# Feed-forward taps that read PSUM, and 33 up-projection blocks multiplied unsplit in fp32 in the first pass

## The chip, the core and the metric

The kernel runs on one core of a Trainium2 chip. The metric is the device time of one execution, in microseconds. A core has five engines with instruction streams of their own: TensorE (PE: matmuls, and PEld: the loads of their stationary operand), VectorE (DVE), ScalarE (ACT), GpSimd (POOL) and SyncE (SP), which here issues all DMAs. TensorE writes its sums to PSUM, in banks of 512 fp32 columns; the other operands stand in SBUF.

## What is computed

One layer of a hybrid decoder for a prompt of 2048 tokens and 8 sample sequences of 8 tokens, all in fp32, with width 1024. A mixing part (convolutions and a gated delta rule) is followed by the feed-forward part that the change is about:

```
up, ffn_buf_new = _causal_dwconv(_rmsnorm(x, norm_ffn_g) @ w_up, ffn_buf, ffn_conv_w, ffn_conv_b)
gate, val = jnp.split(up, 2, axis=-1)
x = x + (jax.nn.silu(gate) * val) @ w_down
```

`w_up` has 1024 x 5632 and `w_down` 2816 x 1024 elements. The causal convolution has 3 taps per channel: `y[t] = w2*u[t] + w1*u[t-1] + w0*u[t-2] + b`, where the two columns ahead of the first are a saved state (zero for the prompt's start).

## The kernel before

**Passes.** The prompt is cut into six passes of 256, 384, 384, 384, 384 and 256 tokens; the last one also carries the 64 sample tokens (320 columns). Activations lie transposed, channels on the 128 partitions and tokens in the columns. Each pass runs its input projection, mixing, `w_out`, norm, feed-forward part and per-layer gate; the mixing of the next pass (convolution steps `cacc`, the delta rule's chain) is merged into the feed-forward stretch of the one before. The position of a unit in that merged plan gives its priority; the final order on each engine and in SP's queue is drawn up when the kernel is built.

**Matmuls.** An fp32 product is made of three fp32r ones: weights and activations are split into a rounded half and the rest, and `gemm` multiplies high by high, high by low and low by high. A block of weights is 8 tiles of 128 x 128, so a `w_up` block takes 24 matmuls into one bank of the pool `g` (three banks), which `w_out`, `w_in`, `w_down` and the PLE gate use too.

**Weights.** `wblock` (L242) brings a block into one of three `w` tiles. The first time it loads it raw (0.5 MB) into a tile `raw`; `split` (L230) lets ScalarE copy the high half and GpSimd (for some `w_in` and `w_out` blocks VectorE) subtract it from the raw one; then the halves (1 MB) are stored to DRAM. Later passes load those halves. Half of the `w_up` and `w_down` blocks aren't stored at the first split but split again in the second pass and stored then (L250). `get` (L260) keeps three blocks ahead.

**Feed-forward.** `units_f` works on 44 blocks of `w_up` per pass, a gate and a value block in turn, and after each four of them on two blocks of `w_down` (four outputs of 128 channels each, 6 matmuls an output) of the group before. In `half` (L1211) GpSimd copies the two saved columns from `ffh` to the head of an SBUF tile `row`; the matmuls fill a bank; ScalarE copies the bank behind those two columns of `row`, and writes `y = w2*u + b` from the bank; GpSimd saves the last two columns of `row` to `ffh`; VectorE adds the two other taps to `y`, each a `scalar_tensor_tensor` of `row`, shifted by a column, with `y`. In the last pass the sample tokens go through a tile `srow` in the same way. `units_norm` (L1177) makes the normed activations: part by part VectorE writes `h`, and `split` turns it into the two halves of `hT2`.

**X.** The residual `X` has two buffers of a tag `X`, which the split input of the second pass also uses early on. Every pass loads its `X` from DRAM in `units_w` (L1161, the load in L1167).

Of the kernel before, what the change touches and what calls it, by code (L numbers as in the profile page):

```python
# [42 lines left out]
def step_kernel(  # L43
# [23 lines left out]
    def nm(s):  # L67
        uid[0] += 1
        return f"{s}_{uid[0]}"
# [10 lines left out]
    def gbank():  # L80
        return pg.tile([P, 512], F32, tag="g", name=nm("g"))
# [65 lines left out]
    def r_tile(tag, w=NMAX, dt=F32):  # L147
        return rp.tile([P, w], dt, tag=tag, name=nm(tag), bufs=3)

    def srow_tile():  # L150
        return rp.tile([P, NSQ, 38], F32, tag="srow", name=nm("srow"), bufs=2)

    def h_tile(name="h"):
        return rp.tile([P, 512], F32, tag="h", name=nm(name), bufs=2)
# [84 lines left out]
    def w_tile():  # L239
        return wp.tile([P, 2, KD, P], F32R, tag="w", name=nm("w"), bufs=3)  # L240

    def wblock(key, src, hi_e="a", lo_e="g", nk=KD):  # L242
        w = w_tile()
        if key in halves:
            SY.dma_start(w.bitcast(F32), halves[key])
        else:
            raw = raw_tile("raw")
            SY.dma_start(raw if nk == KD else raw.rearrange("p (k o) c -> p k (o c)", k=nk), src)
            split(raw, w[:, 0], w[:, 1], hi_e, lo_e)
            if key[0] in ("w_up", "down") and key not in seen and (key[1] // P + key[-1]) % 2:  # L250
                seen.add(key)
                return w[:, 0], w[:, 1]
            halves[key] = hw.tile([P, 2, KD, P], F32, tag=nm("halves"), name=nm("halves"))
            SY.dma_start(halves[key], w.bitcast(F32))
        return w[:, 0], w[:, 1]
# [32 lines left out]
    def halfs(a):  # L288
        return a[:, 0], a[:, 1]

    def gemm_w(ps, w, hT, c0, cw):
        gemm(ps, (lambda k: w[0][:, k, :], lambda k: w[1][:, k, :]),
             (lambda k: hT[0][:, k, c0:c0 + cw], lambda k: hT[1][:, k, c0:c0 + cw]), KD)
# [45 lines left out]
    def to_row(q, row, srow, r, ps, fn):  # L339
        for off, q0, ln in seg(q):  # L340
            if q0 is None:
                fn(srow[:, :, r:r + LSQ], sv(ps[:, off:off + ln]), off, ln)
            else:
                fn(row[:, r:r + ln], ps[:, off:off + ln], off, ln)
# [832 lines left out]
    def units_norm(q):  # L1177
        n = q.n

        def stats():  # L1180
            q.hT2 = big.tile([P, 2, KD, NMAX], F32R, tag="hT2", name=nm("hT2"))
            rs = token_rs(q.acc, q)
            q.dgs = []
            for t, c0, L in q.tiles:
                q.dgs.append(dp.tile([P, P], F32, tag="Zt", name=nm("dg"), bufs=ZB))
                ts(V, q.dgs[-1][:L, :L], ident[:L, :L], rs[:L, t:t + 1], MUL)

        def spread_rs():
            q.nps = ps = bank()
            for i, (t, c0, L) in enumerate(q.tiles):  # L1190
                mm(ps[:, c0:c0 + L], one1[:L, :], q.dgs[i][:L, :L], i == 0, i == len(q.tiles) - 1)

        def part(b):
            h = h_tile()
            stt(V, h[:, :n], q.X[:, b, 0:n], gains[:, b, 1:2], q.nps[:, :n], MUL, MUL)
            split(h[:, :n], q.hT2[:, 0, b, 0:n], q.hT2[:, 1, b, 0:n], "a", "v" if b % 2 else "g")
        return [((), stats), ((), spread_rs)] + [((), lambda b=b: part(b)) for b in range(KD)]


    def units_f(q):  # L1200
        n, np_, sam = q.n, q.np, q.sam
        out = []
        z = {}

        def begin():
            z["f"] = big.tile([P, 2 * FG * 2 * NMAX], F32R, tag="F", name=nm("fbuf"))
            if sam:
                z["st"] = big.tile([P, 2 * FT, 2 * NSQ], F32, tag="zs", name=nm("fst"))
                load_T("fst", [st_ffn[0].rearrange("s r c -> (s r) c")], 2 * DFF, z["st"])

        def half(col):  # L1211
            ffS = W["ff"]
            w = get()
            y = r_tile("y")
            row = r_tile("row", NMAX + 3)
            srow = srow_tile() if sam else None
            G.tensor_copy(row[:, 0:2], ffh[:, col, 0:2])  # L1217
            if sam:
                G.tensor_copy(srow[:, :, 0:2], z["st"][:, col, :].rearrange("p (s r) -> p s r", r=2))
            ps = gbank()  # L1220
            gemm_w(ps[:, :n], w, halfs(q.hT2), 0, n)
            to_row(q, row, srow, 2, ps, lambda o, i, *a: act(o, i))
            act(y[:, :n], ps[:, :n], AF.Identity, scale=ffS[:, col, 2:3], bias=ffS[:, col, 3:4])
            G.tensor_copy(ffh[:, col, 0:2], row[:, np_:np_ + 2])  # L1224
            if sam:
                G.tensor_copy(ffh[:, col, 2:18].rearrange("p (s r) -> p s r", r=2), srow[:, :, 8:10])
            for tap in (1, 0):
                for o, i in taps(q, y, row, srow, tap):
                    stt(V, o, i, ffS[:, col, tap:tap + 1], o, MUL, ADD)
            return y  # L1230

        def ff_ap(slot, hl, j, a, b):
            base = ((slot * FG + j) * 2 + hl) * NMAX
            return z["f"][:, base + a:base + b]

        def gate(f):
            z["g"] = y = half(f)
            act(y[:, :n], y[:, :n], AF.Silu)

        def val(f, slot, j):  # L1240
            y = half(FT + f)
            tt(V, y[:, :n], y[:, :n], z["g"][:, :n], MUL)
            split(y[:, :n], ff_ap(slot, 0, j, 0, n), ff_ap(slot, 1, j, 0, n))

        def down(nk, slot, i):
            w = get()
            m = KD // nk
            for o in range(m):
                ps = bank() if q.ip == 0 and o % 2 else gbank()
                gemm(ps[:, :n], (lambda k: w[0][:, k * m + o, :], lambda k: w[1][:, k * m + o, :]),  # L1250
                     (lambda k: ff_ap(slot, 0, k, 0, n), lambda k: ff_ap(slot, 1, k, 0, n)), nk)
                xs = q.X[:, i * m + o, 0:n]
                tt(V, xs, xs, ps[:, :n], ADD)

        out.append(((), begin))
        pend = []
        for g0 in range(0, FT, FG):
            slot = (g0 // FG) % 2
            nk = min(FG, FT - g0)
            for j in range(nk):  # L1260
                f = g0 + j
                out.append(((("w_up", f * P),), lambda f=f: gate(f)))
                out.append(((("w_up", (FT + f) * P),), lambda f=f, slot=slot, j=j: val(f, slot, j)))
            out += pend
            pend = [((("down", g0, i),), lambda nk=nk, slot=slot, i=i: down(nk, slot, i)) for i in range(nk)]
        return out + pend
# [191 lines left out]
```

## Time and profile before

| | us |
|---|---|
| median of 3 runs | 3202.05 |
| lowest, highest | 3193.27, 3202.27 |
| the profiled execution | 3196.92 |
| its span, first to last instruction | 3195.2 |

The profile is of one execution. The page gives busy time by engine; the trace behind it can be asked for stretches of the span, for groups of instructions by line, shape and operation, for waits and for the order of time. A group's line reads: line of the code, engine, operation, tile written <- tiles read, partitions x columns written <- read, count | busy us, mean ns of one | idle us of the engine before them, and what ended it. L96, L105 and L108 are helper lines (`stt`, `tt`, `act`), so the tiles' names tell instructions apart. The feed-forward stretches of the six passes begin at about 345, 785, 1335, 1852, 2368 and 2884 us. TensorE's granted clock is given as a share of 2.4 GHz, as a mean over its two levels, 1.2 and 2.4 GHz.

### The profile page before, as it was taken

What the parts mean: (1) busy time and instruction counts of PE and PEld (TensorE: products, weight loads), DVE (VectorE), ACT (ScalarE), POOL (GpSimd) and SP (SyncE); (2) the same over time, 40 slices, a digit from 0 to 9 for tenths busy, and PEclk for the clock granted to TensorE, in tenths of its full rate; (3) what the DMA queues carried; (4) which work ended last, traced back from release to release, by engine and by line L of the source; (5) the groups of instructions that cost most, each with busy time, mean ns of one, the idle gap of its engine ahead of it and who ended that gap; (6) DMA issues with size and microseconds to landing.
All of it is one profiled execution on the core that took longest, in us unless ns stands there. A gap on an engine that the chain in (4) does not pass through costs nothing.

```text
span 3195.2 us, 51070 instructions
## 1 busy us (share of the span) xinstructions
PE 2973.2 (93%) x18682; PEld 2900.9 (91%) x18682; DVE 2213.8 (69%) x5378; ACT 1122.4 (35%) x2473; POOL 894.5 (28%) x1518
## 2 busy tenths in 40 slices
PE   5979688777999999999999999999999999998998
PEld 5979678677999998999999999999999999998998
DVE  6986889957669686756757666857577866743443
ACT  4333344334323334422234342223442232323223
POOL 3422576634333432211121121121131121111221
PEclk8989898888999999999999999999999999998999
DMA  7636766667777867667665677665767765666885
GB/s 231 203 118 225 239 194 214 185 214 250 297 251 248 271 231 259 237 240 249 228 220 214 237 253 245 228 239 198 249 242 255 261 241 198 219 222 226 301 293 207
DMA packets 291968, 745.28 MB, mean 233 GB/s; under 512 B 51241, under 2 KB 202282, under 8 KB 216575
## 3 DMA queue, kind: packets, MB, share of 16 engines
q1 hardware_dynamic: 291719, 742.03, 67.9%
q8 instruction: 148, 2.42, 0.3%
q14 instruction: 101, 0.83, 0.1%
HBM read 607.75 MB, written 134.57 MB: 232 GB/s over the span
## 4 chain that ended last, share of the span: by engine, by line
PE 64%; DVE 7%; DMA 3%; ACT 1%; issue 1%; SPq 0%; ACTq 0%; DVEq 0%
PE g L89 57%; PE d L89 3%; PE m L89 2%; DMA w<-halves 2%; DVE h L96 1%; PE d L93 1%; PE m L93 1%; DVE y L96 1%; DVE rt L105 1%; DVE hT L105 0%; DMA out_dram<-yt 0%; DVE cacc L96 0%; DVE sy L96 0%; DVE X L100 0%; DVE X L105 0%
## 5 line engine op out<-in xcount | busy, mean ns | idle before, releaser
L89 PE MATMUL g<-hT,w 128*128 128x384 f32 (+2 forms) x9840 | 1684.6, 329 | 38.7 <-ACT hT L108 9.3
L89 PEld LDWEIGHTS g<-hT,w 128*128 128x128 f32 x9840 | 1600.7, 192 | 49.9 <-ACT hT L108 11.0
L89 PE MATMUL g<-fbuf,w 128*128 128x384 f32 (+2 forms) x2904 | 549.4, 338 | 32.8 <-DVE X L105 15.2
L96 DVE SCALAR_TENSOR_TENSOR y<-row,ffS,y 128x384 f32<-128x384 f32 (+1 forms) x528 | 337.6, 639 | 301.8 <-ACT y L108 275.8
L89 PEld LDWEIGHTS g<-fbuf,w 128*128 128x128 f32 x2904 | 489.7, 194 | 43.3 <-DVE X L105 16.8
L96 DVE SCALAR_TENSOR_TENSOR cacc<-H,cfS,cacc 128x384 f32<-128x384 f32 (+1 forms) x696 | 487.4, 700 | 9.3 <-ACT cacc L108 3.0
L105 DVE TENSOR_TENSOR X<-X,g 128x384 f32<-128x384 f32 (+2 forms) x532 | 276.7, 524 | 228.1 <-PE g L89 225.9
L108 ACT ACTIVATE row<-g 128x384 f32<-128x384 f32 (+1 forms) x336 | 152.4, 454 | 598.5 <-PE g L89 594.2
L105 POOL TENSOR_TENSOR w<-raw,w 128x1024 fp32r<-128x1024 f32 x123 | 307.6, 2502 | 193.4 <-ACT w L108 169.9
L1224 POOL COPY ffh<-row 128x2 f32<-128x2 f32 x264 | 61.9, 235 | 594.4 <-ACT row L108 589.5
L89 PE MATMUL g<-x,w 128*128 128x384 f32 (+2 forms) x1152 | 204.1, 331 | 5.9 <-ACT w L108 4.6
L89 PE MATMUL g<-mx,w 128*128 128x384 f32 (+2 forms) x1152 | 193.9, 327 | 12.3 <-DMA w<-halves 9.5
L89 PEld LDWEIGHTS g<-mx,w 128*128 128x128 f32 x1152 | 186.7, 191 | 15.1 <-issue 4.7
L1217 POOL COPY row<-ffh 128x2 f32<-128x2 f32 x264 | 82.8, 314 | 418.2 <-DVE y L96 312.8
L89 PEld LDWEIGHTS g<-x,w 128*128 128x128 f32 x1152 | 192.1, 195 | 6.7 <-ACT w L108 5.0
L108 ACT ACTIVATE y<-g,ffS 128x384 f32<-128x384 f32 (+2 forms) x264 | 169.3, 641 | 0.1
L108 ACT ACTIVATE w<-raw 128x1024 fp32r<-128x1024 f32 x139 | 146.5, 1055 | 63.3 <-PE g L89 14.9
L105 POOL TENSOR_TENSOR fbuf<-y,fbuf 128x384 fp32r<-128x384 f32 (+2 forms) x132 | 136.4, 1034 | 115.0 <-ACT fbuf L108 111.5
L108 ACT ACTIVATE y<-y 128x384 f32<-128x384 f32 (+2 forms) x132 | 65.7, 498 | 217.7 <-DVE y L96 217.4
L108 ACT ACTIVATE fbuf<-y 128x384 fp32r<-128x384 f32 (+2 forms) x132 | 65.8, 498 | 213.5 <-DVE y L105 213.3
L96 DVE SCALAR_TENSOR_TENSOR H<-row,dnS,H 128x384 f32<-128x384 f32 (+1 forms) x144 | 92.8, 646 | 34.2 <-ACT H L108 33.2
L105 POOL TENSOR_TENSOR y<-row,y 128x256 fp32r<-128x256 f32 x48 | 36.2, 754 | 272.7 <-PE m L89 218.1
(338 smaller groups left out, 3291.1 us busy)
## 6 DMA issues: line engine op xcount, KB each, us to landing
w<-halves SPq DMA_DIRECT2D x477, 1024.0 KB
halves<-w SPq DMA_DIRECT2D x106, 1024.0 KB
raw<-in_w_up_dram SPq DMA_DIRECT2D x66, 512.0 KB
raw<-in_w_down_dram SPq DMA_DIRECT2D x33, 512.0 KB
raw<-in_w_in_dram SPq DMA_DIRECT2D x24, 512.0 KB
xt<-in_x_prompt_dram SPq DMA_DIRECT2D x16, 512.0 KB
xT<-xt SPq DMA_DIRECT2D x16, 512.0 KB
out_dram<-yt SPq DMA_DIRECT2D x16, 512.0 KB
```

The lines of the kernel that those rows point to most:

```text
L89: T.matmul(out, lhsT=lhsT, rhs=rhs, start=start, stop=stop, skip_group_check=skip)
L93: T.transpose(out, in_, ident[:k, :k])
L96: return e.scalar_tensor_tensor(out=out, in0=in0, scalar=scalar, in1=in1, op0=op0, op1=op1)
L105: e.tensor_tensor(out=out, in0=a, in1=b, op=op)
L108: A.activation(out, in_, f, **kw)
L1217: G.tensor_copy(row[:, 0:2], ffh[:, col, 0:2])
L1224: G.tensor_copy(ffh[:, col, 0:2], row[:, np_:np_ + 2])
```

## The change

Three things change together.

- `wblock`: in the first pass the `w_up` blocks whose number isn't a multiple of 4 (33 of 44) are loaded raw into a `w` tile and handed on as they are. The other 11, and all `w_down` blocks, are split and stored in the first pass; those 33 are split and stored in the second. No block is split twice any more.
- `units_norm` and `up_gemm`: in the first pass the normed activations are also kept whole, in a tile `hf` of the tag `X`, and an unsplit block is multiplied with them by 8 fp32 matmuls.
- `half`: the bank holds two more columns ahead of the result, which ScalarE fills from `ffh`. VectorE's taps of the prompt columns read the bank, shifted by a column, and `row` is gone. ScalarE saves the last two columns to `ffh` after the taps. Sample columns still go through `srow`.

```diff
     def wblock(key, src, hi_e="a", lo_e="g", nk=KD):
+        if key[0] == "w_up" and key[1] // P % 4 and key not in seen:
+            seen.add(key)
+            w = wp.tile([P, KD, P], F32, tag="w", name=nm("w"), bufs=3)
+            SY.dma_start(w, src)
+            return w
         w = w_tile()
...
             split(raw, w[:, 0], w[:, 1], hi_e, lo_e)
-            if key[0] in ("w_up", "down") and key not in seen and (key[1] // P + key[-1]) % 2:
-                seen.add(key)
-                return w[:, 0], w[:, 1]
             halves[key] = hw.tile([P, 2, KD, P], F32, tag=nm("halves"), name=nm("halves"))
...
         def part(b):
-            h = h_tile()
+            if q.ip == 0:
+                if b == 0:
+                    q.hf = big.tile([P, KD, n], F32, tag="X", name=nm("hf"), bufs=2)
+                h = q.hf[:, b]
+            else:
+                h = h_tile()
...
+        def up_gemm(ps, w):
+            if isinstance(w, tuple):
+                return gemm_w(ps, w, halfs(q.hT2), 0, n)
+            for k in range(KD):
+                mm(ps, w[:, k, :], q.hf[:, k, :], k == 0, k == KD - 1, skip=False)
+
         def half(col):
             ffS = W["ff"]
             w = get()
             y = r_tile("y")
-            row = r_tile("row", NMAX + 3)
-            srow = srow_tile() if sam else None
-            G.tensor_copy(row[:, 0:2], ffh[:, col, 0:2])
+            ps = gbank()
+            up_gemm(ps[:, 2:2 + n], w)
+            act(ps[:, 0:2], ffh[:, col, 0:2])
+            act(y[:, :n], ps[:, 2:2 + n], AF.Identity, scale=ffS[:, col, 2:3], bias=ffS[:, col, 3:4])
             if sam:
+                srow = srow_tile()
                 G.tensor_copy(srow[:, :, 0:2], z["st"][:, col, :].rearrange("p (s r) -> p s r", r=2))
-            ps = gbank()
-            gemm_w(ps[:, :n], w, halfs(q.hT2), 0, n)
-            to_row(q, row, srow, 2, ps, lambda o, i, *a: act(o, i))
-            act(y[:, :n], ps[:, :n], AF.Identity, scale=ffS[:, col, 2:3], bias=ffS[:, col, 3:4])
-            G.tensor_copy(ffh[:, col, 0:2], row[:, np_:np_ + 2])
-            if sam:
+                act(srow[:, :, 2:2 + LSQ], sv(ps[:, 2 + np_:2 + n]))
                 G.tensor_copy(ffh[:, col, 2:18].rearrange("p (s r) -> p s r", r=2), srow[:, :, 8:10])
             for tap in (1, 0):
-                for o, i in taps(q, y, row, srow, tap):
-                    stt(V, o, i, ffS[:, col, tap:tap + 1], o, MUL, ADD)
+                c = ffS[:, col, tap:tap + 1]
+                stt(V, y[:, 0:np_], ps[:, tap:tap + np_], c, y[:, 0:np_], MUL, ADD)
+                if sam:
+                    stt(V, sv(y[:, np_:n]), srow[:, :, tap:tap + LSQ], c, sv(y[:, np_:n]), MUL, ADD)
+            act(ffh[:, col, 0:2], ps[:, np_:np_ + 2])
             return y
```

## Rows read from the trace of the kernel before

**Rows 1.** The page, busy time by engine: us (share of the span) and instructions.

```profile
PE 2973.2 (93%) x18682; PEld 2900.9 (91%) x18682; DVE 2213.8 (69%) x5378; ACT 1122.4 (35%) x2473; POOL 894.5 (28%) x1518
```

**Rows 2.** Busy time by stretch: us, each engine (instructions), clock, DMA share, GB/s.

```profile
345.00:700.00 355.00, 273.13 (x1910) 259.24 (x1909) 320.23 (x547) 150.00 (x308) 222.98 (x215) 0.88 0.65 201
...
785.00:1224.00 439.00, 418.39 (x2489) 409.77 (x2487) 322.10 (x670) 159.57 (x317) 149.91 (x211) 0.98 0.74 256
...
1335.00:1743.00 408.00, 405.98 (x2465) 401.46 (x2464) 266.00 (x652) 128.86 (x282) 66.98 (x178) 1.00 0.67 233
```

**Rows 3.** Groups by shape in the stretch 345 to 700 us.

```profile
L105 POOL TENSOR_TENSOR w<-raw,w 128x1024 fp32r<-128x1024 f32 x63 | 158.4, 2518 | 38.2 <-ACT w L108 30.1 <-PE g L89 7.6
...
L96 DVE SCALAR_TENSOR_TENSOR cacc<-H,cfS,cacc 128x384 f32<-128x384 f32 x116 | 120.2, 1037 | 1.0
L96 DVE SCALAR_TENSOR_TENSOR y<-row,ffS,y 128x256 f32<-128x256 f32 x88 | 73.2, 831 | 9.0 <-ACT y L108 8.5
...
L105 DVE TENSOR_TENSOR X<-X,g 128x256 f32<-128x256 f32 x44 | 17.9, 410 | 4.8 <-PE g L89 4.8
...
L108 ACT ACTIVATE row<-g 128x256 f32<-128x256 f32 x44 | 16.5, 375 | 18.3 <-PE g L89 18.2
```

**Rows 4.** Groups by shape, VectorE, 1335 to 1743 us.

```profile
L96 DVE SCALAR_TENSOR_TENSOR cacc<-H,cfS,cacc 128x384 f32<-128x384 f32 x116 | 73.4, 632 | 2.0 <-ACT cacc L108 0.8
```

**Rows 5.** Groups by shape, VectorE, 2884 to 3125 us (the last pass).

```profile
L96 DVE SCALAR_TENSOR_TENSOR y<-row,ffS,y 128x256 f32<-128x256 f32 x86 | 42.0, 489 | 77.2 <-ACT y L108 61.1 <-POOL ffh L1226 16.1
```

**Rows 6.** Order of time: start us, us, engine, line, operation, tiles, count [idle before].

```profile
520.20 2.39 POOL L105 TENSOR_TENSOR w<-raw,w 128x1024 fp32r<-128x1024 f32 x1 [1.19 <-ACT w L108]
520.45 2.42 DVE L96 SCALAR_TENSOR_TENSOR y<-row,ffS,y 128x256 f32<-128x256 f32 x1
...
525.00 2.82 PE L89 MATMUL g<-hT,w 128*128 128x256 f32 x22
```

**Rows 7.** Groups by shape, the whole span: operations with a stream in PSUM.

```profile
L96 DVE SCALAR_TENSOR_TENSOR h<-X,gains,m 128x256 f32<-128x256 f32 x8 | 3.7, 478 | 2.0 <-PE m L89 1.1 <-POOL hT L105 0.7
...
L108 ACT ACTIVATE srow<-g 128x64 f32<-128x64 f32 x56 | 12.4, 221 | 0.2 <-DVE y L96 0.2
```

**Rows 8.** The tile kd: count, ns min/median/max, first and last start us, forms.

```profile
L89 PE MATMUL d<-kd,Lm x64: 377/379/767, 80.2 to 2391.1; 128*128 128x256 f32 x64
L105 DVE TENSOR_TENSOR kd<-Um,gg x32: 409/420/2461, 68.9 to 2388.6; 128x256 f32<-128x256 f32 x32
```

**Rows 9.** Order of time on TensorE, 294 to 298 us.

```profile
295.36 0.60 PE L89 MATMUL d<-kd,Lm 128*128 128x256 f32 x2
...
297.54 0.59 PE L89 MATMUL d<-kd,Lm 128*128 128x256 f32 x2
```

**Rows 10.** Waits, 345 to 700 us: engine and tile <- what it waited for: us, times, longest.

```profile
ACT y L108 <- DVE y L96: 60.2, 19, 6.1
...
PE g L89 <- POOL w L105: 11.1, 11, 2.9
```

**Rows 11.** Order of time in the last pass, where a w_down turn begins.

```profile
2974.49 1.92 PE L89 MATMUL g<-fbuf,w 128*128 128x320 f32 x12
...
2975.07 0.62 ACT L108 ACTIVATE y<-g,ffS 128x320 f32<-128x320 f32 x1
...
2975.57 0.49 DVE L105 TENSOR_TENSOR X<-X,g 128x320 f32<-128x320 f32 x1 [2.13 <-PE g L89]
...
2976.37 0.28 DVE L96 SCALAR_TENSOR_TENSOR y<-srow,ffS,y 128x64 f32<-128x64 f32 x1
...
2976.57 0.48 DVE L105 TENSOR_TENSOR X<-X,g 128x320 f32<-128x320 f32 x1
2976.97 0.48 DVE L96 SCALAR_TENSOR_TENSOR y<-row,ffS,y 128x256 f32<-128x256 f32 x1
```

**Rows 12.** Order of time in SP's queue, 293 to 297 us.

```profile
294.10 4.38 SPq L1167 DMA_DIRECT2D X<-xT  x2
```

**Rows 13.** The chain that ended last, in order of time, about 798 us.

```profile
797.97 4.28 DMA raw<-in_w_up_dram
```

## The prediction

> **What bounds the kernel now.** I read the page first: TensorE is busy in 93% of the span [rows 1]. That mean hides two kinds of stage, so I cut the span at the feed-forward stretches of the six passes. In the second and third of them (785 to 1224 us and 1335 to 1743 us) TensorE is busy for 418.4 of 439 us and for 406.0 of 408 us [rows 2]: those stretches last as long as their matmuls, and other engines' savings are worth nothing there unless TensorE waits for them. The first one, 345 to 700 us, is different: TensorE is busy for 273.1 of 355 us and VectorE for 320.2, at a granted clock of 0.88, that is, with part of the time at the lower of the two levels, 1.2 instead of 2.4 GHz [rows 2].
>
> Why is VectorE so busy there? In the groups of this stretch the convolution step of the next pass (cacc) has a mean of 1037 ns and the feed-forward tap (y<-row) one of 831 ns [rows 3]. The same shapes take 632 ns [rows 4] and 489 ns [rows 5] in later stretches, where GpSimd splits no weights. The timeline shows how: a tap that starts 0.25 us after GpSimd's subtraction of a weight split (2.39 us) lasts 2.42 us itself, until that subtraction is over [rows 6]. Not every operation suffers: the 44 additions X<-X,g, with one operand in PSUM, have a mean of 410 ns in the same stretch and none of that [rows 3]. So VectorE operations whose two streams both come from SBUF stand still while GpSimd subtracts, and those with one stream in PSUM don't. This first stretch is where the change acts.
>
> **The change part by part.** Per execution 99 blocks (66 of w_up, 33 of w_down) are loaded raw and 66 stored as halves, as before; the bytes don't change. What moves is who splits when. Before, the first pass splits 44+22 blocks and the second 22+11. After, the first splits 11+22 and the second 33+0. The second pass splits as many as before, and its DMAs are as many; the first pass has 33 splits fewer.
>
> *Stretched VectorE time in the first stretch.* Taps: 88 x (831-489) = 30.1 us. Convolution: 116 x (1037-632) = 47.0 us. Together 77.1 us by 66 splits, 1.17 us for each. With taps that read PSUM and half of the splits, 30.1 + 47.0/2 = 53.6 us go. But a split that now meets a tap may meet a convolution step after; if the 33 that remain stretch as much each, 33 x 1.17 = 38.6 us stay and 38.5 us go. I take the middle, 46 us, and keep both ends.
>
> *The tap itself.* No row shows this tap from PSUM. The nearest is h<-X,gains,m, the same operation with one stream in PSUM: 478 ns at 256 columns [rows 7], against 489 ns for the tap from SBUF [rows 5]. I count no difference. [...]
>
> *Matmuls.* 33 blocks of 24 matmuls become 8 unsplit fp32 products. Split ones: 22 matmuls at 256 columns take 2.82 us [rows 6]; an estimate of 0.28 us for the last one's own duration leaves 2.54/21 = 0.121 us from start to start, 2.9 us for a block. Unsplit fp32 products leave two records each: 32 tiles kd are written and 64 matmuls of 0.379 us read them [rows 8]. Two of these in a row take 0.60 or 0.59 us [rows 9], so 0.22 or 0.21 us from start to start. A block then takes 8 x 2 x 0.215 = 3.44 us: 0.54 us dearer, 33 x 0.54 = +18 us of TensorE. It lies beside VectorE's work: 273.1+18 = 291 us, and VectorE's side, below, still ends later. If that cover is gone, it costs 18 us.
>
> *GpSimd and ScalarE.* In the stretch 33 x 2.52 = 83 us of GpSimd go [rows 3], with ScalarE's copies ahead of them, and GpSimd's two small copies a block go in all passes. ScalarE loses the row copy (375 ns here [rows 3]) and gains two 2-column copies; the nearest row, a 64-column copy from PSUM, is 221 ns [rows 7], so 442 against 375: no difference that counts. TensorE waited for splits on GpSimd for 11.1 us in this stretch [rows 10]; I leave that in the range, since the matmuls that replace it are longer.
>
> *Waits that are added.* ScalarE copies the block's last two columns to ffh after VectorE's second tap, and the bank g is free only after that. Queued behind it on ScalarE are the next evacuations and SiLU; behind the bank is TensorE. In the last pass I follow it through: a w_down turn starts at 2974.49 and each of its outputs takes some 0.88 us, ScalarE's y ends at 2975.69, and the taps and two additions share VectorE [rows 11]. The bank would come free at about 2977.4, after VectorE's second tap of the prompt columns (2976.97 on) and one of the sample columns. The fifth output wants it at 2978.0; the third and fourth take the two other banks as their additions end, 2976.06 and 2977.05, against 2976.3 and 2977.15. It fits with about 0.1 to 0.2 us to spare. 11 such turns in 5 passes are 55; I count 4 us, and 0 to 15 us (0.28 us, one short tap in the way, for each) as the bounds.
>
> *The X buffer.* The unsplit h takes the buffer into which X of the second pass is loaded now at about 295 us, right behind that of the first [rows 12]. That load moves behind the last w_up block of the first pass, in SP's queue among the loads of the w_down and w_out blocks. One transfer of 0.5 MB took 4.28 us [rows 13], and this one is three times as large: some 7 to 13 us, with the last w_down blocks (8 outputs, 24 matmuls each) to hide it. I count nothing; uncovered, it is up to 7 us. Unsplit weights land straight in w: the same 4.28 us, against two blocks (5.8 us) of lead. Nothing, as long as that holds.
>
> **Sum.** The profiled execution took 3196.9 us (3195.2 of span and 1.7 around); the median is 3202.05, 0.16% above. First stretch: VectorE 320.2-46 = 274 us; with its 35 us of idle time kept, 309 instead of 355 us, against TensorE's 291. So -46. Second to sixth: +4. 3196.9-46+4 = **3155 us**.
>
> **The rivals.** *TensorE keeps its idle time.* In the first stretch it has 82 us of it, much behind the chain of the delta rule, which is latency and no load. If what VectorE saves only becomes idle time there, the fp32 matmuls add 18 us and the split waits give 11 us back: 3196.9+4+7 = 3208 at the very worst; halfway between that and the forecast, 3181. For it: TensorE's nominal work rises. Against it: VectorE's idle share is only a tenth.
>
> *Slower: banks wait for late taps.* In the first stretch VectorE lags: ScalarE's SiLU waited for taps 19 times, 60.2 us in all, 6.1 us at the longest [rows 10]. Today that lag doesn't reach TensorE, because a bank is free after ScalarE's two reads. After, the bank is held over the lag, and the copy of two columns waits in ScalarE's queue. It decides where the lag exceeds the two other banks' blocks, 5.8 us. If all of it turned into TensorE waits, +60: 3215. Against it: the lag is itself mostly stretch, which shrinks. [...]
>
> *It doesn't do what it says:* taps stay stretched by GpSimd. Then only the halved number of splits counts, -38.5: 3162, inside the forecast's own range.
>
> *More than forecast.* 53.6 us, the 20.6 us in which TensorE is idle in the second pass (where cacc is stretched too), and the 11.1 us of split waits: 3112.
>
> **Chances.** Forecast with the third rival, 3135 to 3172: 0.52. TensorE's idle time, 3172 to 3196: 0.20, two thirds of it still over 0.3% faster. More than forecast: 0.18, of which 0.04 below 3112. Banks, above 3196: 0.10. A measurement of this kernel tells about 0.3%, 10 us, from no change. Faster 0.83, same 0.07, slower 0.10; range 3112 to 3196.
>
> **What would show it.** In the first feed-forward stretch: y taps with means near 480 ns (right), or 700 and more (third rival); cacc near 800 ns; w<-raw on GpSimd 33 times; unsplit matmuls 528 records with 0.215 us spacing; the stretch some 310 us long. TensorE waits put down to ScalarE's ffh in any pass, or later stretches longer than 408 us, speak for the bank rival. The prediction is wrong if the stretch stays above 340 us, or if a later one grows by over 5 us.

## The result, and the profile after

The changed kernel takes 3147.38 us (median of 4 runs, 3144.97 to 3150.69) where the kernel before took 3202.16 us beside it: a ratio of 0.984, with a 95% interval of 0.9819 to 0.9861. The forecast was 3155 us. Measured once more (`after_again` in the table below) the ratio was 0.9846 [0.9831, 0.986].

The page of the kernel after, busy time by engine as in [rows 1]:

```profile
PE 2968.5 (94%) x18418; PEld 2888.1 (92%) x18418; DVE 2121.8 (67%) x5378; ACT 1074.2 (34%) x2702; POOL 664.2 (21%) x957
```

TensorE's busy time is nearly what it was; VectorE lost 92 us and GpSimd 230. The feed-forward stretches of passes 1, 2, 3 and 4, as in [rows 2] (start:end and length, then busy us of PE, PEld, DVE, ACT and POOL, granted clock, DMA share, GB/s), each cut at its own start and at the first w_out matmul of the next pass:

```profile
342.00:633.00 291.00, 251.79 (x1592) 229.29 (x1591) 246.95 (x541) 117.82 (x317) 112.03 (x99) 0.95 0.75 237
729.00:1193.00 464.00, 440.81 (x2598) 431.83 (x2599) 326.19 (x719) 166.63 (x391) 133.49 (x132) 0.98 0.75 257
1283.00:1709.00 426.00, 424.94 (x2574) 420.68 (x2573) 283.20 (x692) 136.91 (x352) 48.93 (x98) 1.00 0.67 236
1804.00:2231.00 427.00, 425.70 (x2577) 420.81 (x2576) 283.71 (x694) 137.36 (x352) 49.65 (x97) 1.00 0.67 236
```

and the first stretch of the kernel before, cut in the same way, which [rows 2] show with some of the w_out stage behind it:

```profile
349.00:688.00 339.00, 259.21 (x1818) 245.76 (x1818) 313.82 (x530) 148.08 (x304) 222.48 (x215) 0.87 0.64 197
```

The first stretch fell from 339.4 to 290.6 us. That is the change; all other stages together took 2.6 us more than before. Stage by stage, from the starts of the same instructions in both traces (FF is a feed-forward stretch, from ScalarE's first `y` of the pass to the first w_out matmul of the next; w is the stage from there to the next FF; us):

| | start | FF1 | w2 | FF2 | w3 | FF3 | w4 | FF4 | w5 | FF5 | w6 | FF6 and end | span |
|---|---|---|---|---|---|---|---|---|---|---|---|---|---|
| before | 348.7 | 339.4 | 97.5 | 458.8 | 90.3 | 426.3 | 90.7 | 426.3 | 90.0 | 431.1 | 85.2 | 310.8 | 3195.2 |
| after | 342.0 | 290.6 | 96.2 | 463.8 | 89.9 | 426.5 | 95.0 | 427.0 | 94.0 | 431.7 | 84.4 | 307.8 | 3149.0 |

The groups of the first stretch after, which answer to [rows 3]:

```profile
L96 DVE SCALAR_TENSOR_TENSOR cacc<-H,cfS,cacc 128x384 f32<-128x384 f32 x116 | 88.6, 764 | 1.6
L105 POOL TENSOR_TENSOR w<-raw,w 128x1024 fp32r<-128x1024 f32 x32 | 76.8, 2402 | 116.2 <-ACT w L108 112.7 <-PE d L89 2.6 <-POOL T L815 0.7
L96 DVE SCALAR_TENSOR_TENSOR y<-g,ffS,y 128x256 f32<-128x256 f32 x88 | 42.0, 479 | 23.5 <-ACT y L108 22.9
...
L105 DVE TENSOR_TENSOR y<-y,y 128x256 f32<-128x256 f32 x22 | 18.3, 831 | 1.3 <-ACT y L108 1.1
...
L108 ACT ACTIVATE ffh<-g 128x2 f32<-128x2 f32 x44 | 7.5, 170 | 68.3 <-DVE y L96 68.3
```

Taps went from 831 to 479 ns and the convolution step from 1037 to 764. But one operation became slower: the product of gate and value, y<-y,y, took 513 ns before (the line below) and takes 831 now.

```profile
L105 DVE TENSOR_TENSOR y<-y,y 128x256 f32<-128x256 f32 x22 | 11.3, 513 | 0.2
```

The order of time shows what each meets (start us, us, engine, line, operation):

```profile
487.37 2.35 POOL L105 TENSOR_TENSOR w<-raw,w 128x1024 fp32r<-128x1024 f32 x1 [4.77 <-ACT w L108]
...
487.72 1.00 DVE L96 SCALAR_TENSOR_TENSOR y<-g,ffS,y 128x256 f32<-128x256 f32 x2 [0.31 <-ACT y L108]
...
488.76 1.24 DVE L105 TENSOR_TENSOR y<-y,y 128x256 f32<-128x256 f32 x1
...
499.79 2.39 POOL L105 TENSOR_TENSOR w<-raw,w 128x1024 fp32r<-128x1024 f32 x1 [0.72 <-POOL T L815]
500.07 2.39 DVE L105 TENSOR_TENSOR y<-y,y 128x256 f32<-128x256 f32 x1
```

At 487.72 two taps run at full speed while GpSimd subtracts; the product behind them, with both operands in SBUF, stands until GpSimd is done at 489.72. It ends at 490.00, 0.28 us later. At 500.07 the product starts inside a subtraction that ends at 502.18, and it ends at 502.46, again 0.28 us later.

### The profile page after: what moved, and what is told of

The parts are those of the page before. It is cut to its first block, busy times and chain, and to the rows that moved or that the text cites. A ratio compares the mean times of both kernels' runs of the same rounds, so it can differ in the third digit from the quotient of the medians.

```text
span 3149.0 us, 49670 instructions
## 1 busy us (share of the span) xinstructions
PE 2968.5 (94%) x18418; PEld 2888.1 (92%) x18418; DVE 2121.8 (67%) x5378; ACT 1074.2 (34%) x2702; POOL 664.2 (21%) x957
## 4 chain that ended last, share of the span: by engine, by line
PE 65%; DVE 7%; DMA 4%; ACT 1%; issue 1%; POOL 0%; SPq 0%; ACTq 0%; DVEq 0%
PE g L89 57%; PE d L89 3%; DMA w<-halves 3%; PE m L89 2%; PE d L93 1%; DVE h L96 1%; PE m L93 1%; DVE y L96 1%; DMA raw<-in_w_up_dram 1%; DVE cacc L96 0%; DVE H L96 0%; DVE X L100 0%; DVE hT L105 0%; DVE tv L105 0%; DVE X L105 0%
## 5 line engine op out<-in xcount | busy, mean ns | idle before, releaser
L89 PE MATMUL g<-hT,w 128*128 128x384 f32 (+2 forms) x9048 | 1575.3, 332 | 35.6 <-ACT hT L108 9.4
L89 PEld LDWEIGHTS g<-hT,w 128*128 128x128 f32 x9048 | 1499.2, 190 | 46.7 <-ACT hT L108 11.1
L96 DVE SCALAR_TENSOR_TENSOR y<-g,ffS,y 128x384 f32<-128x384 f32 (+1 forms) x528 | 300.7, 570 | 332.3 <-ACT y L108 244.5
L96 DVE SCALAR_TENSOR_TENSOR cacc<-H,cfS,cacc 128x384 f32<-128x384 f32 (+1 forms) x696 | 453.0, 651 | 10.3 <-ACT cacc L108 3.1
L105 POOL TENSOR_TENSOR w<-raw,w 128x1024 fp32r<-128x1024 f32 x90 | 218.6, 2430 | 297.7 <-ACT w L108 284.6
L89 PEld LDWEIGHTS g<-mx,w 128*128 128x128 f32 x1152 | 191.8, 195 | 17.8 <-issue 11.5
L108 ACT ACTIVATE g<-ffh 128x2 f32<-128x2 f32 x264 | 45.7, 173 | 444.0 <-PE g L89 441.8
L89 PEld LDWEIGHTS g<-x,w 128*128 128x128 f32 x1152 | 190.4, 194 | 6.7 <-ACT w L108 5.0
L108 ACT ACTIVATE y<-g,ffS 128x384 f32<-128x384 f32 (+2 forms) x264 | 169.7, 643 | 13.5 <-ACT g L108 0.4
L108 ACT ACTIVATE ffh<-g 128x2 f32<-128x2 f32 x264 | 45.2, 171 | 351.2 <-DVE y L96 351.2
L89 PE MATMUL g<-hf,w 128*128 128x256 f32 x528 | 125.4, 392 | 7.1 <-DMA w<-in_w_up_dram 3.7
L108 ACT ACTIVATE w<-raw 128x1024 fp32r<-128x1024 f32 x106 | 111.6, 1052 | 57.3 <-PE g L89 18.7
L89 PEld LDWEIGHTS g<-hf,w 128*128 128x128 f32 x528 | 101.1, 197 | 21.4 <-DVE X L105 3.3
```

The source lines that it names most:

```text
L89: T.matmul(out, lhsT=lhsT, rhs=rhs, start=start, stop=stop, skip_group_check=skip)
L96: return e.scalar_tensor_tensor(out=out, in0=in0, scalar=scalar, in1=in1, op0=op0, op1=op1)
L105: e.tensor_tensor(out=out, in0=a, in1=b, op=op)
L108: A.activation(out, in_, f, **kw)
```

## The experiments

All ratios are to the kernel before on the same chip, with 95% intervals. Two theories stand against each other on where the gain comes from. A: GpSimd's subtractions stretch VectorE's operations with two streams in SBUF, and the stretch bounds the first feed-forward stretch. B: what bounds it is something else (waits of TensorE, banks, the number of transfers), and the shorter VectorE operations only go with it. Beside that, whether the bank that is held over the taps costs anything. Two profiles of the changed kernel, `after` and `after_again`, differ by 2.8 us in the first stretch and by 2.4 us in w4 + w5, so smaller differences between single profiles say nothing.

**The taps alone.** The kernel before with the new `half` alone; that is the kernel after with `wblock` (its lines below) and the norm as before.

```diff
-        if key[0] == "w_up" and key[1] // P % 4 and key not in seen:
-            ...
+            if key[0] in ("w_up", "down") and key not in seen and (key[1] // P + key[-1]) % 2:
+                seen.add(key)
+                return w[:, 0], w[:, 1]
```

> The kernel before with only the new half: taps read the bank, row is gone, ffh is saved by ScalarE after the taps; weights are split and stored as before (66 splits in the first pass). Theory (GpSimd's subtractions stretch VectorE operations whose two streams are in SBUF, and taps from PSUM are out of it): taps in the first feed-forward stretch have a mean near 480 ns instead of 831; the convolution step stays at 1037 ns or a little more, since 66 splits are still there; VectorE saves some 30 us there, the whole kernel 15 to 30 us: 3172 to 3187. Rival, banks held over late taps: with 66 splits VectorE still lags, TensorE waits for ffh for 20 us and more in that stretch, and the total is 3202 or above. Rival, only the number of splits counts: taps stay near 800 ns, total 3202.

0.9954 [0.9938, 0.997]. The groups of its first stretch, and TensorE's longest sum of waits there (what waits <- for what: us, times, longest):

```profile
L96 DVE SCALAR_TENSOR_TENSOR cacc<-H,cfS,cacc 128x384 f32<-128x384 f32 x116 | 134.9, 1163 | 1.3 <-ACT cacc L108 0.2
...
L96 DVE SCALAR_TENSOR_TENSOR y<-g,ffS,y 128x256 f32<-128x256 f32 x88 | 41.8, 475 | 9.3 <-ACT y L108 6.5 <-ACT g L108 2.5
```

```profile
PE g L89 <- ACT ffh L108: 31.5, 14, 4.9
```

The taps escape, and 31 us of VectorE's time in them go; but cacc rises from 1037 to 1163 ns, and takes 15 us of that back. And TensorE now waits 31.5 us for banks that are released only by the copy to ffh. The stretch falls from 339.4 to 323.1 us, and the whole is inside what the theory expected (3179 us).

**The unsplit blocks alone.** The kernel after, with `half` and its `row` as before.

```diff
-            act(ps[:, 0:2], ffh[:, col, 0:2])
...
+            row = r_tile("row", NMAX + 3)
+            G.tensor_copy(row[:, 0:2], ffh[:, col, 0:2])
...
-                stt(V, y[:, 0:np_], ps[:, tap:tap + np_], c, y[:, 0:np_], MUL, ADD)
+                for o, i in taps(q, y, row, srow, tap):
+                    stt(V, o, i, ffS[:, col, tap:tap + 1], o, MUL, ADD)
```

> The changed kernel with half as before (row in SBUF, GpSimd's two copies), that is 33 unsplit blocks alone. Theory: 33 splits remain in the first pass; taps, again with both streams in SBUF, share what is left of the stretch: mean of taps near 660 ns, of the convolution step near 830 ns, VectorE saves some 35 us in the stretch and the fp32 matmuls (+18 us) stay hidden: 3165 to 3178. The two halves of the change then add up to about the whole (-55 us). Rival, taps from PSUM bring nothing: 3147. Rival, TensorE becomes the bound with fp32 matmuls: 3190 and above.

0.9843 [0.9826, 0.9859], 3147 us, which is all that the whole change gives. The theory had expected 3165 to 3178; this is the number of the rival, by which taps from PSUM bring nothing. Its taps still read SBUF:

```profile
L96 DVE SCALAR_TENSOR_TENSOR cacc<-H,cfS,cacc 128x384 f32<-128x384 f32 x116 | 86.7, 748 | 2.0 <-ACT cacc L108 0.4
...
L96 DVE SCALAR_TENSOR_TENSOR y<-row,ffS,y 128x256 f32<-128x256 f32 x88 | 58.8, 669 | 11.2 <-ACT y L108 10.5
...
L105 DVE TENSOR_TENSOR y<-y,y 128x256 f32<-128x256 f32 x22 | 24.9, 1133 | 0.2
```

The stretch is 294.5 us; with the taps in PSUM as well it is 290.6 (after) and 287.9 (`after_again`). So with half of the splits gone the taps are worth 4 to 7 us there, against 16 us with all of them. The two parts don't add up: alone they give 0.5% and 1.6%, together 1.5 to 1.6%. Part of the reason is the late save, which comes with the new taps: w4 and w5 are 182.4 us together here and 189.0 in the kernel after. The next experiment takes it away.

**The save ahead of the taps.** The kernel after, with one line moved.

```diff
             act(y[:, :n], ps[:, 2:2 + n], AF.Identity, scale=ffS[:, col, 2:3], bias=ffS[:, col, 3:4])
+            act(ffh[:, col, 0:2], ps[:, np_:np_ + 2])
...
-            act(ffh[:, col, 0:2], ps[:, np_:np_ + 2])
             return y
```

> The changed kernel with ScalarE's copy of the last two columns to ffh ahead of the taps instead of behind them; the bank is then free after VectorE's second tap, and ScalarE no longer waits for it. Theory (the wait of ScalarE, 351 us in sum, is mostly off the path): TensorE's waits put down to ffh (6.5 us in the first stretch, 6.2 us in the second) go, the total falls by 3 to 12 us: 3135 to 3144. Rival, the copy's place is worth nothing because TensorE finds another bank free: 3147 within 3 us.

0.9801 [0.9787, 0.9816], beside 0.984 and 0.9846 for the kernel after: 0.4 to 0.5% for one line, 12 to 14 us, somewhat more than the 3 to 12 us expected. Against `unsplit_only` (0.9843) it shows the taps without the late save: 0.4%, and 9.7 us of the first stretch. The group of ScalarE's copy over the whole span, after and then in `save_first`: the engine idled 351.2 us ahead of it for taps, and now doesn't.

```profile
L108 ACT ACTIVATE ffh<-g 128x2 f32<-128x2 f32 x264 | 45.2, 171 | 351.2 <-DVE y L96 351.2
```

```profile
L108 ACT ACTIVATE ffh<-g 128x2 f32<-128x2 f32 x264 | 43.1, 163 | 0.0
```

FF1 falls to 284.8 us (from 290.6 and 287.9), w4 and w5 by 3.6 and 3.1 us, to 91.4 and 90.9, about what they were before the change.

**GpSimd's subtraction on VectorE, nothing else.** The kernel before; the first-time splits of the feed-forward blocks subtract on VectorE. This is the direct test of A against B: VectorE gets 63 operations more in the stretch, and the code of no matmul, transfer or bank changes.

```diff
-            split(raw, w[:, 0], w[:, 1], hi_e, lo_e)
+            first = key[0] in ("w_up", "down") and key not in seen2
+            seen2.add(key)
+            split(raw, w[:, 0], w[:, 1], hi_e, "v" if first else lo_e)
```

> The kernel before, in which the first split of each w_up and w_down block (66 in the first pass) subtracts on VectorE instead of GpSimd; the second splits stay on GpSimd. Theory (GpSimd's subtraction is what stretches VectorE): in the first feed-forward stretch the convolution step falls from 1037 to near 632 ns and the tap from 831 to near 489 ns, while VectorE pays 66 x 1.22 = 81 us for the subtractions; with some 77 to 109 us of stretch gone, the total is between 3170 and 3205. Rival (something else stretches them, DMA traffic or ScalarE): the means stay, VectorE has 81 us more, the total is 3260 or more.

0.9818 [0.9804, 0.9833], 3136 us: at least as fast as the whole change. The theory had the direction but not the size: it expected 3170 to 3205, with 77 to 109 us of stretch gone. Its first stretch:

```profile
L105 DVE TENSOR_TENSOR w<-raw,w 128x1024 fp32r<-128x1024 f32 x63 | 77.6, 1233 | 12.6 <-ACT w L108 11.3 <-PE g L89 1.3
L96 DVE SCALAR_TENSOR_TENSOR cacc<-H,cfS,cacc 128x384 f32<-128x384 f32 x116 | 75.1, 648 | 1.0 <-ACT cacc L108 0.8
...
L96 DVE SCALAR_TENSOR_TENSOR y<-row,ffS,y 128x256 f32<-128x256 f32 x88 | 41.4, 479 | 5.3 <-ACT y L108 5.2
```

```profile
350.00:638.00 288.00, 233.65 (x1830) 223.62 (x1829) 265.35 (x591) 149.81 (x303) 98.74 (x150) 0.93 0.73 233
```

VectorE does 77.6 us of subtractions more, and is busy for 265 us instead of 314. Of theory B's terms, the waits of TensorE for split weights could have fallen too, but they didn't: 18.0 us before (GpSimd's 11.1 [rows 10] and the first line below), 17.8 now (the other two). Nor did VectorE wait for GpSimd in either stretch.

```profile
PE g L89 <- ACT w L108: 6.9, 7, 2.3
```

```profile
PE g L89 <- ACT w L108: 10.7, 6, 5.1
PE g L89 <- DVE w L105: 7.1, 11, 1.3
```

So theory B doesn't explain the 52 us that the stretch lost. Half of them are idle time of TensorE (80 to 54 us) and half its busy time (259 to 234 us, for as many matmuls), at a granted clock of 0.93 instead of 0.87; that the clock rose because TensorE waits less isn't tested apart. Summed by duration, VectorE's operations other than the subtractions fall from 348.0 to 229.1 us: 118.9 us by 63 splits, 1.9 us for each subtraction of 2.52 us that leaves GpSimd. Taps and cacc are 76 us of it, as the prediction had them; the other 43 are many small groups that it didn't count (the largest, zf<-zf,tv and tv<-zf, 8 us each). On VectorE the subtraction costs 1.23 us.

**How much for each split.** One condition of the diff changed: all 44, or 22, `w_up` blocks unsplit in the first pass instead of 33.

```diff
-        if key[0] == "w_up" and key[1] // P % 4 and key not in seen:
+        if key[0] == "w_up" and key not in seen:                 # unsplit_44
+        if key[0] == "w_up" and key[1] // P % 2 and key not in seen:  # unsplit_22
```

> The changed kernel with all 44 w_up blocks unsplit in the first pass (22 splits left there, 44 in the second). Theory: 11 splits fewer take some 10 us more of stretch from VectorE, 11 x 0.54 = 6 us go onto TensorE; in the first stretch VectorE is no longer the bound alone, so the stretch changes by -8 to +4 us; in the second pass 11 more splits stretch VectorE, where TensorE is the bound: 0 to +6 us. Total 3141 to 3155. Rival, the number of splits sets the first stretch alone: 3130.

> The changed kernel with every second w_up block unsplit in the first pass (22; 44 splits left there, 22 in the second). Theory: 11 splits more in the first stretch cost VectorE 11 x 1.2 = 13 us of stretch, TensorE has 6 us less; in the second pass 11 splits fewer. Total 3147 to 3162. Rival, TensorE sets the first stretch: 3141.

0.9793 [0.9779, 0.9808] and 0.9834 [0.9817, 0.9851]; both are below what the theory expected (3127 us against 3141 to 3155, and 3145 against 3147 to 3162), and the first is near its rival's 3130, by which the number of splits sets the stretch alone. With the taps in PSUM the first stretch is 323.1, 301.8, 290.6 and 272.2 us for 66, 44, 33 and 22 splits: 0.97, 1.01 and 1.67 us a split, on average 1.16; the last two, over 11 splits each, are uncertain by some 0.25 us through the 2.8 us between two profiles alone. The whole time doesn't follow as plainly, since the blocks that aren't split in the first pass are split in the second: FF2 was 446.8, 463.8 and 458.4 us for 22, 33 and 44 of them. It is not in the order of their number, and no run here tells why.

**44 unsplit, with the early save.** Both of the single improvements together.

> All 44 w_up blocks unsplit in the first pass, and ffh saved ahead of the taps. Theory: the two gains have different places (first stretch; the w_out stages of the fourth and fifth pass and ScalarE's waits) and add up: 3127 less 8 to 16 us, 3111 to 3121, the best so far. Rival: both shorten the same waits, the total stays at 3127 within 4 us.

0.9803 [0.9787, 0.9819], no better than either: the gains don't add up, as the rival had it. w4 and w5 fell by 6.7 us (188.9 to 182.1), but the first stretch gained nothing (275.0 against 272.2 us; TensorE is busy for 253 us of it), and w2 is 108.5 us, against 103.4 in `unsplit_44` and 96.2 in the kernel after. So the early save is worth 0.4 to 0.5% beside 33 unsplit blocks, and nothing over the whole beside 44.

**Taps in PSUM without GpSimd's splits.** `before_dve_split` with the `half` of the kernel after (late save).

> The kernel before with the first splits of w_up and w_down on VectorE (as before_dve_split) and the new half (taps from the bank). No subtraction on GpSimd is left in the first stretch. Theory, taps from PSUM are worth only the stretch that they escape: tap 479 ns in both, so the total is that of before_dve_split (3135) within 6 us, perhaps some us more for the w_out stages. Rival, they have a worth of their own (no row copy, no GpSimd copies, an earlier y): 3125 or less.

0.9851 [0.9837, 0.9866], slower than `before_dve_split` (0.9818): 10 us, where the theory expected 6 at most and perhaps some more for the w_out stages. Where nothing stretches, taps that read PSUM leave VectorE as busy as before (265 us). The stretch is 3 us shorter, but TensorE waits there 13.5 us for the late save, and w4 and w5 are 7.4 us longer together.

```profile
PE g L89 <- ACT ffh L108: 13.5, 11, 4.3
```

**What remains moved to VectorE.** `save_first`, and `split44_save_first`, with the splits that remain in the first pass (33 and 22) subtracted on VectorE.

```diff
-            split(raw, w[:, 0], w[:, 1], hi_e, lo_e)
+            split(raw, w[:, 0], w[:, 1], hi_e, "v" if key[0] in ("w_up", "down") and key not in seen else lo_e)
```

> The changed kernel with ScalarE's copy to ffh moved ahead of the taps, as in save_first, and with the subtraction of the 33 feed-forward splits that remain in the first pass on VectorE instead of GpSimd. In before_dve_split VectorE's busy time in the first stretch fell from 314.8 to 264.9 us although 63 subtractions of 1.23 us were added, so each split on GpSimd had cost VectorE about 2.0 us. Theory (GpSimd's subtraction stretches VectorE's operations with two SBUF streams): 32 x (2.0-1.23) = 25 us less VectorE time than in save_first, about 225 us; TensorE, 254 us busy, is then the longer one, and the stretch falls from 285 to about 270 us: ratio to the kernel before about 0.975. cacc about 640 ns. Rival (with taps in PSUM and half of the splits gone the stretch no longer decides; TensorE's own waits do): cacc falls in the same way, but the stretch stays within 280 to 290 us, ratio 0.979 to 0.982.

> As unsplit33_save_dve, but with all 44 up-projection blocks unsplit in the first pass; only the 22 down-projection blocks are split there, on VectorE. It is split44_save_first with those subtractions moved off GpSimd. The first stretch of split44_save_first (275.0 us) had TensorE busy for 253 us, so little is left there: 265 to 275 us. Its second w_out stage had grown to 108.5 us from 95 to 97. If that growth comes from GpSimd's splits of the stretch before, it shrinks to below 100 us here, and the ratio is about 0.973; if it comes from the 44 splits of the second pass or from the order of the transfers, it stays at 103 to 109 us, and the ratio is about 0.979.

0.9775 [0.9747, 0.9804] and 0.9756 [0.9741, 0.9771]. The second is the fastest kernel here: 3116.56 us, 0.9% below the changed kernel by the ratios. Its first stretch:

```profile
339.00:606.00 267.00, 251.93 (x1529) 228.80 (x1528) 227.19 (x567) 109.30 (x309) 38.89 (x67) 0.99 0.70 219
```

TensorE is busy for 252 of 267 us, at a granted clock of 0.99 (0.87 before): the stretch has come close to the later ones, bound by its matmuls. With 33 unsplit the stretch took 276.5 us, between what the two theories expected, as VectorE fell to 237 and not to 225 us: each split took only about 1.4 us of stretch with it here ((279.3 - 273.2 + 39.0)/32, from summed durations), fewer operations being left to stretch. w2 is still 104.2 us with 44 splits in the second pass, and 98.3 with 33. So its growth doesn't come from GpSimd's splits of the first pass; it comes with 44 blocks left to the second pass (103.4 to 108.5 us in three kernels, against 95.2 to 98.3 with 22 or 33), by a path that these runs don't separate.

All kernels side by side (FF1 with its busy times, mean ns of cacc and of the tap there; w4 + w5 are two later w_out stages):

| | ratio | FF1, us | PE | DVE | cacc | tap | w4 + w5, us | save |
|---|---|---|---|---|---|---|---|---|
| before | 1 | 339.4 | 259 | 314 | 1037 | 831 | 180.8 | GpSimd |
| taps_only | 0.9954 | 323.1 | 253 | 300 | 1163 | 475 | 190.4 | late |
| unsplit_only | 0.9843 | 294.5 | 251 | 258 | 748 | 669 | 182.4 | GpSimd |
| after | 0.984 | 290.6 | 252 | 247 | 764 | 479 | 189.0 | late |
| after_again | 0.9846 | 287.9 | 251 | 247 | 746 | 478 | 186.6 | late |
| save_first | 0.9801 | 284.8 | 254 | 249 | 746 | 479 | 182.3 | early |
| unsplit_22 | 0.9834 | 301.8 | 255 | 255 | 819 | 479 | 190.7 | late |
| unsplit_44 | 0.9793 | 272.2 | 257 | 234 | 713 | 480 | 188.9 | late |
| split44_save_first | 0.9803 | 275.0 | 253 | 232 | 717 | 479 | 182.1 | early |
| before_dve_split | 0.9818 | 287.6 | 234 | 265 | 648 | 479 | 182.6 | GpSimd |
| taps_dve_split | 0.9851 | 284.5 | 237 | 265 | 641 | 474 | 190.0 | late |
| unsplit33_save_dve | 0.9775 | 276.5 | 254 | 237 | 639 | 477 | 181.4 | early |
| unsplit44_save_dve | 0.9756 | 266.5 | 252 | 227 | 621 | 478 | 181.9 | early |

Read the last two columns together: w4 + w5 is 186.6 to 190.7 us in every kernel with the late save and 180.8 to 182.6 in every other. A part of it is seen in SP's queue, at the start of w4 of the kernel after and of `save_first`:

```profile
1709.25 0.32 SPq L250 DMA_DIRECT2D w<-halves  x1
1718.77 0.56 SPq L399 DMA_DIRECT2D xT<-xt  x1
1720.91 2.75 SPq L250 DMA_DIRECT2D w<-halves  x3
```

```profile
1700.07 0.32 SPq L250 DMA_DIRECT2D w<-halves  x1
1707.22 0.56 SPq L399 DMA_DIRECT2D xT<-xt  x1
1710.05 4.13 SPq L250 DMA_DIRECT2D w<-halves  x3
```

The store of xt, a part of the next pass's input norm, stands in the queue ahead of three loads of weights; with the late save it leaves 9.5 us after the load in front of it, with the early one 7.2 us, and the first of the weights behind it leaves 11.7 and 10.0 us after that load. The waits of TensorE's w_out matmuls over the whole span, before (first line), after (second) and in `save_first` (third):

```profile
L89 PE MATMUL g<-mx,w 128*128 128x384 f32 x768 | 136.9, 337 | 5.8 <-DMA w<-halves 5.3 <-DVE mx L105 0.3 <-issue 0.2
```

```profile
L89 PE MATMUL g<-mx,w 128*128 128x384 f32 x768 | 142.9, 347 | 11.3 <-DMA w<-halves 11.3
```

```profile
L89 PE MATMUL g<-mx,w 128*128 128x384 f32 x768 | 137.3, 338 | 2.8 <-DMA w<-halves 1.8 <-DVE pT L105 1.0
```

In the kernel after, 5.2 of the 11.3 us for weights stand at the start of w2; the rest is one wait in w4 and one in w5:

```profile
PE g L89 <- DMA w<-halves: 2.8, 1, 2.8
...
PE g L89 <- DMA w<-halves: 3.3, 1, 3.3
```

Together they are 6.1 us, against 1.5 before and 1.4 in `save_first`: 4.7 of the 6.7 us between the kernel after and `save_first`. That the late save brings the longer stages about is shown by the table, six measurements against seven; by which step of the order that is drawn up when the kernel is built, isn't.

## Why the prediction was right, point by point

**The bound, and the first stretch: right.** -46 us was forecast for it and -48.8 came; over the profiled executions it was -42 and -46.2. That GpSimd's subtraction was the cause is shown by `before_dve_split`, which takes away nothing else. The kernel after shows it side by side: inside the subtraction of 487.37 to 489.72 us two taps with one stream in PSUM took 1.00 us together, and the product behind them, with both in SBUF, took 1.24 us and ended 0.28 us after it. Why the product is held, no run here tells.

**The price of a split: right as a mean, counted from too little.** 1.17 us was taken from two shapes; the stretch fell by 1.16 us a split between 66 and 22 of them. But a split costs VectorE 1.9 us in `before_dve_split`, over all its operations. VectorE's busy time fell by 67 us, not by 46, and its idle time in the stretch rose from 25 to 44 us, where the sum had kept it: the two errors nearly cancel, and that the stretch came out so close is in part luck.

**The tap in PSUM: right in its price; the late save took its worth back.** It takes 479 ns in the stretch. Where nothing disturbs it, it takes as long as from SBUF, here at 256 columns in the last pass of the kernel after, against 489 ns [rows 5].

```profile
L96 DVE SCALAR_TENSOR_TENSOR y<-g,ffS,y 128x256 f32<-128x256 f32 x88 | 42.3, 481 | 83.4 <-ACT srow L108 83.3
```

The middle of 38.5 and 53.6 us gave the taps 7.5 us beyond the splits. In the change they gave 4 to 7 us in the stretch and nothing over the kernel (0.9843 without them, 0.984 and 0.9846 with); with the early save, 9.7 us in the stretch and 0.4% over the kernel (0.9801). So the number was near for the taps by themselves, and the held bank, below, took it back. The prediction's caution, that a split which misses a tap meets something else, happened as well: it named cacc; it was cacc in `taps_only` (1037 to 1163 ns) and the product in the kernel after (513 to 831 ns).

**The fp32 matmuls: right in their price, not in what lies beside them.** 16 records run in 3.67 us; without the last one's own 0.39 us (the mean of the group) that is 0.219 us from start to start, 0.215 forecast; from the starts of all of them the median is 0.216. The median of the split ones in the first stretch is 0.117, not 0.121 (the last one's own duration, estimated at 0.28 us, is 0.280 us in the median there), so a block is dearer by 0.65 us and not 0.54, 21 us for the 33.

```profile
444.84 3.67 PE L89 MATMUL g<-hf,w 128*128 128x256 f32 x16
```

The sum then had TensorE 18 us busier, under a VectorE that still ends later. Instead TensorE's busy time in the stretch fell from 259 to 252 us, and it is now busier than VectorE (247). The granted clock rose there from 0.87 to 0.95, and matmuls that are the same in both kernels took less time (before, then after):

```profile
L89 PE MATMUL g<-fbuf,w 128*128 128x256 f32 x264 | 57.1, 342 | 24.2 <-DVE X L105 12.2 <-ACT y L108 7.7 <-POOL w L105 4.1
```

```profile
L89 PE MATMUL g<-fbuf,w 128*128 128x256 f32 x264 | 43.4, 302 | 16.6 <-ACT w L108 8.3 <-ACT ffh L108 6.8 <-DVE X L105 1.0
```

The sum had no term for this. That the dearer matmuls stayed covered is therefore not only VectorE's doing; how much of it is the clock's, no run separates.

**The held bank: inside its bounds, but mis-sized and in the wrong place.** +4 us was forecast, 0 to 15 the bounds, at the turns to w_down in passes 2 to 6. What the late save costs is 12 to 14 us, by `save_first`. FF3 to FF5 grew by 0.2 to 0.7 us only, so at these turns the margin held. The cost came in the first stretch (FF1 is 3.0 to 5.8 us shorter with the early save; TensorE waits there 7.1 us for ffh) and in w4 and w5, 4.3 to 6.7 us over the two, in part by way of SP's queue, which the prediction hadn't followed for this edit. As the mechanism of a rival it was real: `taps_only` shows it at 31.5 us of waits. With half of the splits gone the waits were 7.1 us, as was argued from the lag being mostly stretch.

```profile
PE g L89 <- ACT ffh L108: 7.1, 5, 3.8
PE g L89 <- DMA w<-halves: 5.2, 1, 5.2
```

**The X buffer: right.** The load of X moved from 294 to 601 us, and w2 as a whole is 1.3 us shorter than before. At the end of the stretch one wait for a w_out block is 5.2 us long (second line above); `save_first` loads X as late and has no such wait, so it isn't shown to be X's doing.

```profile
601.31 0.34 SPq L1169 DMA_DIRECT2D X<-xT  x1
```

**Not forecast at all:** 6.7 us ahead of FF1, which come with the unsplit blocks (342.6 us in `unsplit_only`, 351.2 in `taps_only`, 348.7 before), and +5.0 us in FF2, which come with them too (466.5 and 460.0, against 458.8). They nearly cancel. The second stands right at the 5 us in a later stretch that the prediction had named as a sign of being wrong. It isn't the bank rival that it was to show, since the new `half` with its late save brings 1.2 us alone (`taps_only`) and the unsplit blocks alone 7.7; but that the second pass would stay as it was, because it splits as many blocks, was wrong, and no run here tells why. Of the rivals, "TensorE keeps its idle time" is out, with 39 us idle in the stretch after against 80 before; "doesn't do what it says" is out by the tap's 479 ns.

## What to carry to other kernels

Where VectorE's operations have long means while GpSimd works, price GpSimd's instruction by what it stretches, over all groups and not the worst two, and try it on VectorE itself first: here 1.23 us there replaced 1.9 us of stretch. Taking one group of operations out of reach passes a part of the stretch on to the next (15 of 31 us in `taps_only`), so such gains don't add up. And when a buffer's last reader moves behind another engine's work, look for an order in which it reads first: here one line was worth 0.4 to 0.5%, as much as the taps had brought.

## What the runs showed of the hardware

A VectorE operation with both streams in SBUF that starts inside a GpSimd subtraction ends shortly after that subtraction, whenever it started: in the first stretch of the changed kernel, all eleven of 384 columns (cacc and its last step, into H) that start at least 0.05 us into one and 0.6 us before its end finish 0.41 to 0.42 us after it, and all seven products y<-y,y of 256 columns 0.28 to 0.29 us after it (so 0.42 us became up to 2.57). The taps with a stream in PSUM passed undisturbed (two in 1.00 us in the middle of a subtraction; 479 ns in the mean of the stretch's 88, 481 in the last pass). A 128x1024 fp32 subtraction takes 2.40 us on GpSimd (after) and 1.23 on VectorE (`before_dve_split`). An fp32 matmul of 256 columns leaves two records 0.216 us apart, and one of fp32r a single record, 0.117 us from the next (medians): an unsplit product costs 16 of the one where the split one costs 24 of the other. The granted clock has two levels in the records, 0.50 and 1.00 of full speed (kernel before: 0.50 over 415 to 420 us, 1.00 over 1335 to 1743 us). At the lower one fp32r matmuls start 0.213 us apart at 256 columns and 0.320 us at 384, 1.2 columns a ns, at the upper one 0.117 and 0.175 us (medians, kernel before). The records name no GHz: 1.2 and 2.4 for the two levels are an estimate from the 1.2 columns a ns, if a column takes a cycle, and from the ratio of the levels. In the first stretch the clock, a mean over the two, stood higher where TensorE idled less: 0.87 before with 80 us idle, 0.93 in `before_dve_split` with 54, 0.95 after with 39, and 0.99 in the fastest kernel with 15; not strictly, since `unsplit_44` had 0.96 with 15.
